# Loading x ahead of the modulation weights, and transposing it two channel tiles ahead of its use

## The chip, the cores and the metric

The kernel runs on one core of one Trainium2 chip. The metric is device time in microseconds (us) of one execution. Below, PE is the matmul engine, DVE, ACT and POOL are the vector, scalar and general engines, and SP is the queue that issues nearly all DMAs.

## The reference, cut to what matters

One layer of an encoder over 512 tokens of 2048 channels, all in float32, with one conditioning vector c:

```python
mod = silu(c) @ w_ada + b_ada                  # 2048 x 12288
sh1, sc1, gt1, sh2, sc2, gt2 = split(mod, 6)
h = rmsnorm(x, g_norm_mix) * (1 + sc1) + sh1
proj = h @ w_in                                # 2048 x 3072: xr, gr (gate), xp (pool)
...                                            # RG-LRU heads and pooling heads, then w_out
x = x + gt1 * y
...                                            # SwiGLU with sh2, sc2, gt2, then a last rmsnorm
```

rmsnorm divides each token's row by the root of its mean square (a factor rstd per token) and multiplies by a weight per channel.

## The kernel before

**How it is written and ordered.** The program lists its operations in order of the mathematics; a class `Program` records them and orders them itself. It gives every operation a cost (`cost`, line 113) and a due time, counted back from the nominal times of PE's matmuls (`deadlines`, line 154), and then places them one by one (`schedule`, line 204): for each engine queue it looks at the operations that are ready, takes the one that can start earliest (due time decides between equal ones), and moves this queue's clock. What is issued is the list in order of the planned starts. Each engine works through its own part of the list in order. All instructions are issued from line 356, so every row of the trace has that line; tiles tell them apart.

Tiles come from pools with a fixed number of buffers: `blk` (names b..., 69 buffers of 128 x 512), `raw` (6) for other weights, `araw` (4 buffers of 512 KB) for the modulation weights, `hi` and `lo` (3 each), and the PSUM banks `acc` (6) and `mm` (2). Buffers of a pool are taken in the program's order; one tile may be taken early only where the rest still fits (`fits`, line 239). Two rules keep buffers free: a `raw` load whose due time lies more than 50 us ahead of its queue's clock is not placed, and far-off operations leave 6 `blk` buffers spare (`buffers`, line 260). DMAs with a `lead` are issued first, in order of the lead.

**The start, around the change.** x is loaded in 16 pieces (four token tiles by four column quarters, `xs[t][q]`, line 466). ACT squares each piece and sums it into `ss1`; from this, DVE and ACT form `rstd1`, one factor per token (line 470). ACT then multiplies each piece by rstd1 in place (line 476), PE transposes it in 128 x 128 blocks against the identity into an `acc` bank, and ACT copies the bank to `xt[k]`, a channel tile of 128 channels by 512 tokens (lines 472 to 479). All 16 channel tiles are done so, one after another, before anything else of the mixer in the program's order.

Scale and shift come from w_ada in nine chunks of one or two channel tiles (`ADA_CHUNKS`, `ada_columns`, line 516): each chunk is 2 or 4 MB through the `araw` buffers; DVE multiplies by c's column and adds up (one instruction per 128 x 256 or 128 x 512, `b<-araw,c_act,b`), PE sums over the partitions by matmuls with a column of ones (`mm<-ones,b`), and DVE writes `gs` and `sh`. `shifted(k)` (line 491) applies them to xt[k] and splits the result into a float32r high part and a low part, h[k]; all products run as three float32r matmuls (high by high, high by low, low by high).

With h[k], PE computes the input projection over the columns in two ways: six column tiles stay in the six `acc` banks over all chunks (`held_job`, line 573, sums over all 16 channel tiles), ten others are summed in groups of channel tiles 0 to 1, 2 to 7 and 8 to 15 through the two `mm` banks (`group_job`, line 583). The eight gate columns follow after the last chunk. The loop over chunks is at lines 749 to 769.

Of the kernel before, what the change touches and what calls it, by code (L numbers as in the profile page):

```python
# [12 lines left out]
AF = mybir.ActivationFunctionType  # L13
ALU = mybir.AluOpType

P = 128
D = 2048
T = 512
NT = T // P
KD = D // P  # L20
# [7 lines left out]
ADA_CHUNKS = (1, 1, 2, 2, 2, 2, 2, 2, 2)  # L28
GROUP_ENDS = (2, 8, 16)
HELD = 6  # L30
NFF = 5632 // 512
DOWN_BLOCKS = (2, 3, 3, 3)
BUFS = {"blk": 69, "raw": 6, "araw": 4, "hi": 3, "lo": 3, "acc": 6, "mm": 2}
# [3 lines left out]
class Program:  # L37
# [166 lines left out]
    def schedule(self):  # L204
        self.dependences()
        self.deadlines()
        ops, tags, bufs = self.ops, self.tags, self.bufs
# [19 lines left out]
        taken, last_use = set(), {}  # L227
        waiting, ready = [len(op["pred"]) for op in ops], [0.0] * len(ops)
        clock = {q: 0.0 for q in self.QUEUES.values()}
        dma_free, table, busy, port = 0.0, None, {}, 0.0  # L230
        start, left = [None] * len(ops), len(ops)
        pace = [op for op in ops if op["q"] == "PE"][::-1]
        shift, wide = 0.0, False
# [26 lines left out]
        def buffers(op, now):  # L260

            need, when = [x[0] for x in op["w"] if x[0] in tags and x[0] not in taken], 0.0
            for name in need:
                tag = tags[name]
                late = op["due"] - shift - now
                if not free[tag] or tag == "raw" and late > self.RAW_AHEAD and not wide:
                    return need, None
                if not fits(name, self.spare.get(tag, 0) if late > self.SPARE_AHEAD else 0):
                    return need, None
                when = max(when, min(free[tag]))  # L270
            return need, when
# [7 lines left out]
        while left:  # L279
            while pace and start[pace[-1]["i"]] is not None:  # L280
                pace.pop()
            shift = pace[-1]["nominal"] - clock["PE"] if pace else shift
            best = {}
            for (q, _), heap in lanes.items():
                now, tried = clock[q], []
                while heap and (wide or len(tried) < self.SCAN):
                    due, i = heapq.heappop(heap)
                    tried.append((due, i))
                    if q == "PE" and pace and ops[i]["nominal"] > pace[-1]["nominal"] + self.AHEAD:
                        continue  # L290
                    need, when = buffers(ops[i], now)
                    if when is None:
                        continue
                    t = max(now, ready[i], when, port if ops[i]["port"] else 0.0)
                    cand = (t, due + 2.0 * (ops[i]["table"] not in (None, table)), i, need)
                    if q not in best or t < best[q][0] - 0.02 or t <= best[q][0] + 0.02 and cand[1] < best[q][1]:
                        best[q] = cand
                    if t <= now and ops[i]["table"] in (None, table):
                        break
                for x in tried:  # L300
                    heapq.heappush(heap, x)
            if not best:
                assert not wide, "no instruction can go"
                wide = True
                continue
            wide = False
            t, _, i, need = min(best.values())
            op = ops[i]
            q = op["q"]
            heap = lanes[lane(op)]  # L310
            heap.remove((op["due"], i))
            heapq.heapify(heap)
            for name in need:
                tag = tags[name]
                free[tag].remove(max([x for x in free[tag] if x <= t] or free[tag]))
                taken.add(name)
                early[tag].append(place[name])
            start[i] = t
            if op["dma"]:
                issue = self.DMA_ISSUE if q == "SP" else self.DMA_BUILD  # L320
                clock[q] = t + issue
                dma_free = max(dma_free, t + issue + self.DMA_START - self.DMA_ISSUE) + op["t"]
                end = dma_free + self.DMA_LAND
            else:
                if op["table"] not in (None, table):
                    t, table = t + self.TABLE_LOAD, op["table"]
                    start[i] = t
                end = t + op["t"]
                if op["port"]:
                    port = max(port, end)  # L330
                if q == "PE":
                    tick = int(t / self.CLOCK_TICK)
                    if busy.get(tick - 1, 0.0) < self.CLOCK_SHARE * self.CLOCK_TICK:
                        end += op["t"]
                    busy[tick] = busy.get(tick, 0.0) + op["stream"]
                clock[q] = end
            op["end"] = end
            left -= 1
            for name in op["tiles"]:
                users[name] -= 1  # L340
                last_use[name] = max(last_use.get(name, 0.0), end + self.LATENCY[q])
                if not users[name]:
                    free[tags[name]].append(last_use[name])
            for j in op["succ"]:
                waiting[j] -= 1
                r = ops[j]["q"]
                ready[j] = max(ready[j], end + (0.0 if r == q == "PE" else self.LATENCY[q] + 0.1 * (r == "PE")))
                if not waiting[j]:
                    push(ops[j])
# [10 lines left out]
def hybrid_trunk(ctx: ExitStack, tc: tile.TileContext, a: dict, out: bass.AP):  # L360
# [6 lines left out]
    nc = Program(tc.nc, BUFS, SPARE)  # L367
    ids = iter(range(1 << 20))
    ts, tt, stt = nc.vector.tensor_scalar, nc.vector.tensor_tensor, nc.vector.scalar_tensor_tensor

    def blk(dt=F32):
        return nc.tile(pool, [P, T], dt, "blk", f"b{next(ids)}")
# [5 lines left out]
    def mmps(tag="mm"):  # L378
        return nc.tile(psum, [P, 512], F32, tag, f"{tag}{next(ids)}")
# [30 lines left out]
    ident = const.tile([P, P], F32, name="ident")  # L410
# [8 lines left out]
    def rows_of(src):  # L419
        return src.rearrange("(r p) -> r p", p=P)  # L420
# [37 lines left out]
    x2 = a["x"][0]  # L458
    xs = [[None] * 4 for _ in range(NT)]
# [3 lines left out]
    for q in range(4):  # L463
        for t in range(NT):
            xs[t][q] = blk()
            nc.sync.dma_start(out=xs[t][q], in_=x2[t * P:(t + 1) * P, q * 512:(q + 1) * 512], lead=(0, 2, 4, 6)[q])
            ss = ss1[:, 4 * t + q:4 * t + q + 1]
            nc.scalar.activation(out=blk(), in_=xs[t][q], func=AF.Square, accum_out=ss)

    rstd1 = rstd_from(ss1, NT, after=sqrt_ready)  # L470
    xt = []
    for k in range(KD):
        ps = mmps("acc")
        for t in range(NT):
            if k % 4 == 0:
                nc.scalar.activation(out=xs[t][k // 4], in_=xs[t][k // 4], func=AF.Copy, scale=rstd1[:, t:t + 1])
            nc.tensor.transpose(out=ps[:, t * P:(t + 1) * P], in_=xs[t][k // 4][:, (k % 4) * P:(k % 4 + 1) * P], identity=ident)
        xt.append(blk())
        nc.scalar.activation(out=xt[k], in_=ps, func=AF.Copy)

# [86 lines left out]
    proj = {}  # L567
    held = {n: mmps("acc") for n in range(HELD)}

# [145 lines left out]
    def pool_group(g):  # L715
# [16 lines left out]
        for j in range(2):  # L732
            ps = mmps()
            for k in range(2):
# [11 lines left out]
                  lead=3)  # L746
    start = 0
    group = 0
    for ci, nk in enumerate(ADA_CHUNKS):
        ada_columns(0, start, nk)  # L750
        end = start + nk
        for k in range(start, end):
            h[k] = shifted(k)
        if end == 8:
            param_columns(cols_b, 72,
                          [a["w_conv"][0].rearrange("i (r p) -> (i r) p", p=P), rows_of(a["b_conv"][0]), rows_of(a["b_rg_a"][0]),
                           rows_of(a["b_rg_i"][0]), rows_of(a["lru_lambda"][0]), a["ls_pool"][0].rearrange("g (r p) -> (g r) p", p=P)])
            sp, spn = softplus()
            bd = [gate_weights(name) for name in ("w_rg_a", "w_rg_i")]
        for n0 in range(0, HELD, 8 // nk):  # L760
            held_job(start, nk, n0, min(8 // nk, HELD - n0))
        if end in GROUP_ENDS and end < KD:
            gk = end - group
            m = max(1, 8 // gk)
            for base, cnt in ((HELD, NL - HELD), (2 * NL, NL)):
                for n0 in range(base, base + cnt, m):
                    group_job(group, gk, n0, min(m, base + cnt - n0))
            group = end
        start = end
# [34 lines left out]
    for q in range(4):  # L804
# [18 lines left out]
        for k in range(4 * q, 4 * q + 4):  # L823
            ps = mmps()
# [148 lines left out]
    wd = a["w_ffn_down"][0].rearrange("(ko p) n -> p ko n", p=P)  # L973
    f_kept = [dram.tile([P, 7 * T], F32, name=f"f{i}") for i in range(2 * NFF)]
    gt2_kept = [dram.tile([P, 512], F32, name=f"gt2_{q}") for q in range(4)]
# [60 lines left out]

    for n in range(NFF):
        keep(n, gate_up(n))
# [146 lines left out]
```

## Time and profile before

| | us |
|---|---|
| median of 3 runs | 1902.73 (1899.97 to 1902.89) |
| profiled execution | 1899.48 |
| its span, first to last instruction | 1897.7 |
| PE busy | 1805.7 (95%) |
| DVE busy | 1544.1 (81%) |
| ACT busy | 930.7 (49%) |
| mean granted PE clock | 0.990 |

The profile is of one execution. Busy time counts instructions; matmuls are pipelined and overlap in it. A row of the timeline gives the start, the time covered and the count of a run of like instructions, and in brackets the engine's idle time before it with what ended it.

### The profile page before, as it was taken

To read this page: it belongs to the slowest core of one execution; us is meant where nothing else is said; L and a number is where in the kernel's file an instruction comes from. 1 tells how busy PE (TensorE), PEld (TensorE's weight loads), DVE (VectorE), ACT (ScalarE), POOL (GpSimd) and SP (SyncE) were. 2 spreads that over 40 slices of the span, in tenths; PEclk is the share of its full clock that TensorE was granted. 3 is DMA by queue.
4 is the path that set the end of the run, shared out by engine and by line. 5 is a ranking of instruction groups with operands and counts; after the bars stand their busy time and mean duration, and the time that the engine had idled before them with its cause. 6 is when DMAs were issued, how large, how long until landed. Compare 5 with 4: busy or idle time off the path is not lost.

```text
span 1897.7 us, 22755 instructions
## 1 busy us (share of the span) xinstructions
PE 1805.7 (95%) x8019; PEld 1471.6 (78%) x8019; DVE 1544.1 (81%) x1978; ACT 930.7 (49%) x1208; POOL 197.8 (10%) x192
## 2 busy tenths in 40 slices
PE   3899999899998999999999999999999999999997
PEld 2687877687776788888888888888887888888875
DVE  5897999889969879687877867877667888888888
ACT  7435784432228455454554545545444543333345
POOL 0000045500000111111111111111110000000011
PEclk9999999999999999999999999999999999999999
DMA  9997455599972688678967878867799765947566
GB/s 295 311 350 231 153 180 178 183 318 313 349 240 47 175 205 233 173 227 220 224 186 211 230 183 218 229 175 198 168 288 355 230 237 184 351 142 254 203 158 166
DMA packets 283587, 425.78 MB, mean 224 GB/s; under 512 B 20632, under 2 KB 119632, under 8 KB 283472
## 3 DMA queue, kind: packets, MB, share of 16 engines
q1 hardware_dynamic: 257232, 373.98, 58.9%
q0 software_dynamic: 26240, 50.34, 15.9%
q8 instruction: 63, 1.03, 0.2%
q14 instruction: 52, 0.43, 0.1%
HBM read 374.44 MB, written 49.81 MB: 224 GB/s over the span
## 4 chain that ended last, share of the span: by engine, by line
PE 73%; DVE 13%; DMA 8%; ACT 3%; issue 3%; SPq 0%; POOL 0%; ACTq 0%; DVEq 0%
PE acc L356 70%; DVE b L356 9%; DMA araw<-in_w_ada 4%; PE mm L356 3%; DVE lo L356 3%; ACT b L356 2%; DMA raw<-in_w_ffn_down 1%; ACT hi L356 1%; DMA raw<-in_w_ffn_up 1%; DMA f<-b 1%; DMA raw<-in_w_ada 1%; DVE araw L356 0%; SPq L356 0%; DMA b<-f 0%; DMA raw<-in_w_in 0%
## 5 line engine op out<-in xcount | busy, mean ns | idle before, releaser
L356 PE MATMUL acc<-hi,b 128*128 128x512 f32 x4208 | 1270.0, 392 | 12.7 <-DVE b L356 6.0
L356 PEld LDWEIGHTS acc<-hi,b 128*128 128x128 f32 x4208 | 789.0, 188 | 179.8 <-DVE b L356 9.1
L356 PE MATMUL acc<-lo,b 128*128 128x512 f32 x2104 | 780.7, 392 | 2.3 <-DVE lo L356 2.3
L356 ACT ACTIVATE hi<-raw 128x1024 fp32r<-128x1024 f32 (+2 forms) x289 | 298.6, 1034 | 472.5 <-PE acc L356 405.1
L356 PEld LDWEIGHTS acc<-lo,b 128*128 128x128 f32 x2104 | 396.1, 188 | 89.5 <-DVE lo L356 8.2
L356 DVE TENSOR_TENSOR lo<-raw,hi 128x1024 fp32r<-128x1024 f32 (+2 forms) x289 | 346.0, 1199 | 135.8 <-ACT hi L356 134.7
L356 ACT ACTIVATE hi<-araw 128x1024 fp32r<-128x1024 f32 x264 | 279.5, 1060 | 282.7 <-PE acc L356 254.5
L356 DVE TENSOR_TENSOR lo<-araw,hi 128x1024 fp32r<-128x1024 f32 x198 | 241.3, 1220 | 54.0 <-ACT hi L356 53.2
L356 DVE SCALAR_TENSOR_TENSOR b<-araw,c_act,b 128x512 f32<-128x512 f32 (+1 forms) x315 | 236.1, 755 | 15.7 <-DMA araw<-in_w_ada 11.3
L356 DVE TENSOR_TENSOR b<-b,b 128x512 f32<-128x512 f32 (+4 forms) x318 | 188.5, 617 | 14.6 <-ACT b L356 14.0
L356 PE MATMUL acc<-b,hi 128*128 128x512 f32 x608 | 188.2, 394 | 5.1 <-ACT b L356 4.4
L356 ACT ACTIVATE b<-b 128x512 fp32r<-128x512 f32 (+2 forms) x223 | 128.7, 595 | 92.4 <-DVE b L356 55.3
L356 PEld LDWEIGHTS acc<-b,hi 128*128 128x128 f32 x608 | 114.1, 189 | 30.7 <-ACT b L356 6.5
L356 POOL DMA_DIRECT2D araw<-in_w_ffn_up x44 | 52.6, 1195 | 621.1 <-DVE lo L356 620.3
L356 PE MATMUL acc<-b,lo 128*128 128x512 f32 x304 | 115.0, 392 | 0.0
L356 ACT ACTIVATE b<-acc 128x512 f32<-128x512 f32 x142 | 82.3, 593 | 56.6 <-PE acc L356 45.9
L356 DVE SCALAR_TENSOR_TENSOR lo<-araw,hi 128x1024 fp32r<-128x1024 f32 x66 | 80.6, 1221 | 36.0 <-ACT hi L356 35.6
L356 DVE TENSOR_TENSOR araw<-araw,raw 128x1024 f32<-128x1024 f32 x88 | 106.6, 1218 | 0.8
L356 DVE SCALAR_TENSOR_TENSOR araw<-araw,raw 128x1024 f32<-128x1024 f32 x66 | 79.8, 1219 | 8.8 <-DMA raw<-in_w_ffn_down 4.5
L356 POOL DMA_DIRECT2D raw<-in_w_ffn_up x44 | 52.5, 1192 | 312.9 <-DVE lo L356 284.9
L356 PE MATMUL mm<-b,hi 128*128 128x512 f32 x192 | 62.8, 408 | 12.3 <-ACT b L356 10.9
L356 DVE TENSOR_TENSOR b<-acc,b 128x512 f32<-128x512 f32 x94 | 61.5, 684 | 15.9 <-PE acc L356 15.7
(75 smaller groups left out, 878.8 us busy)
## 6 DMA issues: line engine op xcount, KB each, us to landing
araw<-in_w_ada SPq DMA_DIRECT2D x256, 256.0 KB, 4.6
raw<-in_w_ffn_down SPq DMA_DIRECT2D x88, 512.0 KB, 5.6
f<-b SPq DMA_DIRECT2D x154, 256.0 KB, 4.1
b<-f SPq DMA_DIRECT2D x154, 256.0 KB, 6.1
raw<-in_w_ffn_up SPq DMA_DIRECT2D x44, 512.0 KB, 4.4
araw<-in_w_ffn_gate SPq DMA_DIRECT2D x44, 512.0 KB, 3.9
araw<-in_w_ffn_up POOLq DMA_DIRECT2D x44, 512.0 KB, 6.7
raw<-in_w_ffn_gate SPq DMA_DIRECT2D x44, 512.0 KB, 5.0
```

The source lines that it names most:

```text
L356: getattr(getattr(self.nc, queue), method)(*args, **kw)
```

## The change

x's last column quarter gets a lead of 4.5 instead of 6, so that it is issued before the first modulation weights (lead 5). The transposes become a function `transposed(k)`, which takes an `mm` bank and is called in the loop over chunks, for all channel tiles up to two beyond the chunk's end. For the first eight channel tiles, x is not scaled first: DVE builds four diagonal blocks of rstd1 (`diag`), and the transpose is a matmul of the unscaled block with the diagonal. The other eight are scaled by ACT and transposed as before. In `schedule`, the clock against which a buffer's lead is counted is at least the latest start placed so far (`today`).

```diff
+XT_AHEAD = 2
+DIAG_TILES = 8
...
-        dma_free, table, busy, port = 0.0, None, {}, 0.0
+        dma_free, table, busy, port, today = 0.0, None, {}, 0.0, 0.0
...
-                    need, when = buffers(ops[i], now)
+                    need, when = buffers(ops[i], max(now, today))
...
             t, _, i, need = min(best.values())
+            today = max(today, t)
...
-            nc.sync.dma_start(out=xs[t][q], in_=x2[t * P:(t + 1) * P, q * 512:(q + 1) * 512], lead=(0, 2, 4, 6)[q])
+            nc.sync.dma_start(out=xs[t][q], in_=x2[t * P:(t + 1) * P, q * 512:(q + 1) * 512], lead=(0, 2, 4, 4.5)[q])
...
     xt = []
-    for k in range(KD):
-        ps = mmps("acc")
+
+    diag = blk()
+    for t in range(NT):
+        ts(out=diag[:, t * P:(t + 1) * P], in0=ident, scalar1=rstd1[:, t:t + 1], scalar2=None, op0=ALU.mult)
+
+    def transposed(k):
+
+        ps = mmps()
         for t in range(NT):
+            tok, x = slice(t * P, (t + 1) * P), xs[t][k // 4]
+            if k < DIAG_TILES:
+                nc.tensor.matmul(ps[:, tok], x[:, (k % 4) * P:(k % 4 + 1) * P], diag[:, tok], start=True, stop=True)
+                continue
             if k % 4 == 0:
-                nc.scalar.activation(out=xs[t][k // 4], in_=xs[t][k // 4], func=AF.Copy, scale=rstd1[:, t:t + 1])
-            nc.tensor.transpose(out=ps[:, t * P:(t + 1) * P], in_=xs[t][k // 4][:, (k % 4) * P:(k % 4 + 1) * P], identity=ident)
+                nc.scalar.activation(out=x, in_=x, func=AF.Copy, scale=rstd1[:, t:t + 1])
+            nc.tensor.transpose(out=ps[:, tok], in_=x[:, (k % 4) * P:(k % 4 + 1) * P], identity=ident)
         xt.append(blk())
         nc.scalar.activation(out=xt[k], in_=ps, func=AF.Copy)
...
         ada_columns(0, start, nk)
         end = start + nk
+        for k in range(len(xt), min(KD, end + XT_AHEAD)):
+            transposed(k)
         for k in range(start, end):
             h[k] = shifted(k)
```

## Rows read from the trace of the kernel before

**Rows 1.** The page's 40 slices of the span, busy tenths of PE.
```profile
PE   3899999899998999999999999999999999999997
```

**Rows 2.** Busy time (instructions) by stretch; last: granted clock, DMA share, GB/s.
```profile
26.00:41.40 15.40, 10.02 (x54) 8.07 (x55) 12.10 (x35) 13.56 (x27) 0.00 (x0) 0.97 1.10 375
41.40:57.00 15.60, 12.20 (x52) 8.00 (x50) 13.30 (x20) 10.09 (x18) 0.00 (x0) 0.92 0.91 284
57.00:79.00 22.00, 19.76 (x82) 15.13 (x83) 18.25 (x30) 10.27 (x17) 0.00 (x0) 0.92 1.01 334
79.00:97.50 18.50, 17.63 (x81) 13.85 (x80) 18.43 (x32) 10.25 (x17) 0.00 (x0) 1.00 0.99 299
97.50:147.80 50.30, 50.30 (x224) 41.27 (x224) 47.96 (x87) 14.88 (x22) 0.00 (x0) 1.00 1.02 341
147.80:151.50 3.70, 1.03 (x9) 0.97 (x8) 3.70 (x10) 2.08 (x4) 0.00 (x0) 1.00 0.99 331
151.50:183.00 31.50, 31.49 (x146) 26.21 (x147) 22.03 (x50) 15.59 (x24) 0.00 (x0) 1.00 0.74 239
```
The order of the five engines in each row is PE, PE's weight loads, DVE, ACT, POOL.

**Rows 3.** Timeline of the SP queue, 11 to 21 us.
```profile
11.42 7.40 SPq L356 DMA_DIRECT2D araw<-in_w_ada  x8
18.86 2.07 SPq L356 DMA_DIRECT2D b<-in_x  x4
```

**Rows 4.** Timeline of PE, 34 to 99 us.
```profile
34.68 1.61 PE L356 MATMUL acc<-ident,b 128*128 128x128 f32 x12 [0.17 <-ACT b L356]
...
41.70 1.20 PE L356 MATMUL acc<-b,hi 128*128 128x512 f32 x2
...
57.13 0.50 PE L356 MATMUL mm<-b,lo 128*128 128x512 f32 x1 [2.70 <-DVE lo L356]
...
93.41 1.02 PE L356 MATMUL mm<-ones,b 128*128 128x1 f32 x8 [0.20 <-DVE b L356]
...
97.50 1.43 PE L356 MATMUL acc<-b,hi 128*128 128x512 f32 x5
```

**Rows 5.** Groups of ACT, 29 to 50 us: busy, mean ns of one, idle before.
```profile
L356 ACT ACTIVATE b<-b,s 128x512 f32<-128x512 f32 x16 | 10.2, 714 | 0.0
L356 ACT ACTIVATE b<-acc 128x512 f32<-128x512 f32 x16 | 8.7, 606 | 0.0
...
L356 ACT ACTIVATE b<-b,sh,gs 128x512 fp32r<-128x512 f32 x1 | 0.8, 813 | 0.0
```

**Rows 6.** The chain of waits that ended last: start, us, what.
```profile
79.59 2.95 DMA araw<-in_w_ada
...
141.64 4.76 DMA araw<-in_w_ada
```

**Rows 7.** Timeline of DVE, 18 to 79 us.
```profile
18.22 0.35 DVE L356 TENSOR_SCALAR b<-araw,c_act 128x256 f32<-128x256 f32 x1 [5.51 <-DMA araw<-in_w_ada]
...
29.41 0.15 DVE L356 SCALAR_TENSOR_TENSOR gs<-gs,cols_a 128x1 f32<-128x1 f32 x1
...
75.20 0.16 DVE L356 TENSOR_TENSOR gs<-mm,cols_a 128x2 f32<-128x2 f32 x1 [1.08 <-PE mm L356]
...
78.68 0.16 DVE L356 TENSOR_TENSOR gs<-mm,cols_a 128x2 f32<-128x2 f32 x1 [1.02 <-PE mm L356]
```

**Rows 8.** Instructions on the tile ident: least, median, greatest ns; first and last.
```profile
L356 DVE TENSOR_SCALAR b<-ident,s x4: 281/285/288, 553.0 to 565.5; 128x128 f32<-128x128 f32 x4
```

**Rows 9.** Timeline of PE near 567 us, a f32 matmul of 128 columns.
```profile
567.22 1.91 PE L356 MATMUL mm<-b,ones 128*128 128x128 f32 x8
```

**Rows 10.** Timeline of PE, 147 to 153 us.
```profile
148.80 1.02 PE L356 MATMUL mm<-ones,b 128*128 128x1 f32 x8 [0.99 <-DVE sh L356]
151.51 1.66 PE L356 MATMUL acc<-b,hi 128*128 128x512 f32 x6 [1.69 <-ACT b L356]
```

**Rows 11.** Busy time by stretch, columns as in rows 2, two later stretches.
```profile
500.00:600.00 100.00, 88.62 (x400) 70.31 (x399) 83.08 (x157) 51.01 (x89) 4.92 (x4) 0.95 0.66 207
...
1800.00:1898.00 98.00, 82.16 (x351) 66.23 (x349) 83.80 (x117) 47.62 (x75) 13.66 (x16) 0.94 0.64 164
```

## The prediction

> **What bounds the kernel now.** I read the page first, for its 40 slices [rows 1]: PE is at 3 tenths in the first slice, then at 8 or 9 of 10 nearly everywhere. What the change touches directly lies in the first four slices, so the next view is the table of busy time by stretch, cut where the PE's work changes its kind [rows 2]. The reader is to see three things in it. First, from 97.5 to 147.8 PE is busy for all of 50.30 us, and from 151.5 to 183 for 31.49 of 31.50: behind 97.5 PE is full. Second, from 57 to 97.5 DVE is nearly as full: 18.25 of 22.00 us, then 18.43 of 18.50. Third, the DMA share is about 1 from 57 to 147.8 (1.01, 0.99, 1.02). So in the first 150 us two streams run beside each other: PE's products, and the stream of the modulation weights (DMA into four araw buffers, DVE's multiply-adds out of them). DVE gives the buffer back, and the next load waits for that.
>
> Then the timelines. The SP queue [rows 3] issues the first eight ada loads at 11.42 and the last four loads of x only at 18.86, so the row scales of all of x are late. PE [rows 4] transposes x before and after 34.68 (this row is a stretch of it without waits, 12 in 1.61 us) and starts its first projection product at 41.70. ACT in the same stretch [rows 5] carries sixteen scaled copies of x, 10.2 us, and evictions of the transposes; it is the engine that holds the transposes back.
>
> The rows that decide what an earlier start is worth come later: at 93.41 PE waits 0.20 us for DVE's sum of the fifth chunk (channel tiles 6 and 7; I number chunks from one), and at 97.50 it goes on with products [rows 4]. From 97.50 on it has work without a break. So PE comes to that point with no backlog: whatever it does earlier than now, it must wait there, unless the fifth chunk comes earlier too. The chain of waits says the same: from 79.59 to 97 it runs over ada loads and DVE, not over PE, and it comes by an ada load again at 141.64 [rows 6].
>
> **The change, part by part.** All sums are made against the profiled execution, 1899.48 us (span 1897.7, 1.8 us around it). The runs shown have a median of 1902.73, 3.25 above; I add the differences to the median. About 0.2%, 3.8 us, is what a measurement can tell from no change.
>
> *x ahead of the ada weights.* Four DMAs of x, 2.07 us of the SP queue, go ahead of eight ada DMAs of 7.40 us [rows 3]. x's squares end some 7 us earlier (18.86 becomes 11.42). Behind them on SP, the first chunk comes 2.07 us later; DVE's first multiply-add starts at about 20.3 instead of 18.22 [rows 7]. The number of loads is the same, and by the end of the second chunk the queue has issued the same bytes. DVE idles 3.3 us in 26 to 41.4 (15.40 less 12.10, [rows 2]), which covers the 2.07 us. Cost 0; without that cover +2.07.
>
> *rstd as a diagonal.* DVE gets four instructions of 0.285 us, as for the diagonal that the kernel builds later [rows 8], 1.14 us; with the 2.07 us this makes 3.2, just inside the 3.3 us of idle time. Cost 0, bounds 0 and +1.14. ACT loses eight of its sixteen scaled copies, 8 x 0.714 = 5.7 us [rows 5]. No gain by itself: ACT is not what is late behind 52 us (10.27 of 22.00 us busy, [rows 2]). PE pays: 32 transposes become matmuls with a 128-column f32 operand. The nearest row has eight of these in 1.91 us, 0.239 each, against 0.134 for a transpose [rows 4, 9]: 32 x 0.105 = 3.4 us. They fall before 92 us, where PE idles 3.4 + 2.2 + 0.9 us from 41.4 to 97.5 [rows 2] and more before, so I take 0; bounds 0 and +3.4.
>
> The Trainium skill, Perfetto Trace Analysis, section Transposes, wants a logical transpose issued as a transpose and not as a standard matmul. The rows agree on the price (0.134 against 0.239 us); by the rule the change would be 3.4 us dearer, a sum of 1905.1, if PE were late there.
>
> *Transposes just in time, over the two mm banks.* Tiles 0 to 2 are transposed for the first chunk instead of all sixteen, and the six acc banks need not be given back by transposes first. The first product needs gs of the first chunk (29.41 + 0.15 now [rows 7], about 31.6 with 2.07 added) and ACT's 0.81 us [rows 5]: about 33 instead of 41.70, so PE starts 8 to 9 us earlier.
>
> Where does that go? From 57 to 79 the chain is PE's (group products through the two mm banks); DVE waits at 75.20 and 78.68 for PE, 1.08 and 1.02 us [rows 7], and in all idles 3.75 us there (22.00 less 18.25). PE ahead by 8 us takes these waits away. Next late is DVE itself: no multiply-add of the ada chunks goes away. So the fifth chunk comes earlier by 0 to 3.75 us; the stretch right after it, where DVE runs at 18.43 of 18.50 with the DMA at 0.99, shows that it can run without such waits, so I take 3.75. The other idle time, 2.3 us in 41.4 to 57, waits for ada loads, which the change does not speed: 0 there, upper bound 2.3.
>
> Against it stands what the moved transposes cost. Tiles 8 to 15 are now transposed behind 93 us, where PE is full: 8 x 4 x 0.134 = 4.3 us. Two of the eight can go into the hole from 147.8 to 151.5, where PE idles 3.70 less 1.03 = 2.67 us while it waits for DVE and ACT [rows 2, 10]; one more can go early into the wait for the fifth chunk, since one mm bank is free then. Five stay: 5 x 0.535 = 2.7 us. Bounds 0 (all in waits) and 4.3. Their evictions (0.606 us each, [rows 5]) run on ACT, which is busy for only 14.88 of 50.30 us there [rows 2].
>
> *The planner's clock.* It lets a queue that stood still count its lead from the latest instruction placed. It can only change the order of loads and of buffer use. PE's idle time outside the start is small and gives the bounds: 11.4 us in 500 to 600 and 15.8 in the last 98 us [rows 11]. I see no reason for a sign: 0, with 3 us either way, a quarter of the first of these.
>
> Sum: -3.75 + 2.7 = -1.05 us, 1902.73 - 1.05 = 1901.7. That is within 0.2%.
>
> **Rivals.** (1) The early start goes through. All DVE idle time before the fifth chunk vanishes (3.75 + 2.3 us), the hole of 2.67 us closes, and the eight tiles fit into waits: -8.7 us, about 1894. For it: DMA moved 375 GB/s from 26 to 41.4 against 284 from 41.4 to 57 [rows 2], so the loads have room once ACT and DVE are rid of the transposes. Against it: DVE's work stays, 49.98 us of the 56.1 from 41.4 to 97.5, and it would have to run without a gap.
>
> (2) Slower: the transposes decide. If the fifth chunk does not come earlier (DVE is late by x's 2.07 us and never makes up for it), all eight late tiles stay on a full PE, 4.3 us. On top, PE, now ahead, idles before the fifth chunk; after its idle 2.70 us at 57.13 [rows 4] the granted clock of 57 to 79 is 0.92, 8% of 22 us = 1.8 us, for stretches at the lower of its levels. Together +6.1, 1908.8. It decides as soon as the fifth chunk gains less than 2.3 us (6.1 less 3.8). With the diagonal's 3.4 us on the path too it would be 1912.2; of this rival's chance that is 0.04. The Trainium skill's rule on transposes (above) speaks for this side; the trace agrees with its price, and shows no full PE where the diagonal falls.
>
> (3) The re-planned order moves a later stretch by some 6 us, twice the bound taken, either way: 1896 or 1908. The page speaks against much of it, since PE is at 9 tenths in nearly all later slices [rows 1].
>
> **Chances.** Forecast 0.45 (within 0.2%: 0.37; its ends beyond: 0.05 faster, 0.03 slower). Rival 1 0.28, all faster. Rival 2 0.17, all slower. Rival 3 0.10: 0.04 faster, 0.02 within, 0.04 slower. So faster 0.37, same 0.39, slower 0.24. The forecast's own terms go from -6.05 (late tiles all in waits, ada waits gone too) to +4.3, 1896.7 to 1907.0; to leave out no more than 2 in 10, the range takes in most of rivals 1 and 2: 1893 to 1908.5.
>
> **What would show it.** Right: the first product at 33 to 34 us; ada loads starting near 13.5; DVE's waits for PE at 75 to 79 gone; PE idle for several us before the fifth chunk, whose sum reaches PE 2 to 4 us before 93.41; transposes among PE's products behind 93 us; the 500th and the 1400th us showing the same work within 3 us. Wrong: the fifth chunk earlier by more than 6 us, or not at all; PE waiting for an mm bank behind a transpose; the hole near 148 us gone; or the shift at 200 us not being the shift at the end, which would put the cause into the later order.

## The result and the profile after

The changed kernel takes 1914.25 us (median of 5 runs, 1908.98 to 1916.21); the kernel before, run beside it, 1902.89 (1899.97 to 1908.44). The ratio is 1.0053, 95% interval 1.0027 to 1.0079: slower by some 10 us, where no change was forecast and 1908.5 was the upper end. The profiled execution took 1913.98 us with a span of 1912.2, 14.5 more than the span before, so single profiles overstate the loss by a few us. I use the profiles for places and the ratios for sizes.

The SP queue of the changed kernel, 8 to 33 us (start, time covered, count), answers to [rows 3]:

```profile
8.90 4.83 SPq L359 DMA_DIRECT2D b<-in_x  x8
13.78 8.77 SPq L359 DMA_DIRECT2D araw<-in_w_ada  x8
22.59 2.15 SPq L359 DMA_DIRECT2D raw<-in_w_in  x4
24.86 1.39 SPq L359 DMA_DIRECT2D araw<-in_w_ada  x2
...
```

Eight ada loads fill the four araw buffers. Before, x's last four loads then stood in the queue while DVE worked its way to the first free buffer, and the ninth ada load went out at 21.05. Now x is gone from there, four w_in loads stand in that place, and the ninth ada load goes out at 24.86.

DVE's timeline (with the idle time before a row and what ended it): the first multiply-adds of the first six chunks, the reduction for rstd1 that stands ahead of them, one of the splits of w_in between them, and the longest wait on an ada load, in the second chunk; answers to [rows 7].

```profile
20.98 0.17 DVE L359 TENSOR_REDUCE s<-s 128x4 f32<-128x16 f32 x1 [8.46 <-ACT b L359]
...
21.79 0.35 DVE L359 TENSOR_SCALAR b<-araw,c_act 128x256 f32<-128x256 f32 x1
...
30.61 0.96 DVE L359 TENSOR_TENSOR lo<-raw,hi 128x768 fp32r<-128x768 f32 x1 [0.48 <-ACT hi L359]
...
33.28 0.35 DVE L359 TENSOR_SCALAR b<-araw,c_act 128x256 f32<-128x256 f32 x1 [0.33 <-DMA araw<-in_w_ada]
...
42.37 1.52 DVE L359 SCALAR_TENSOR_TENSOR b<-araw,c_act,b 128x256 f32<-128x256 f32 x3 [2.08 <-DMA araw<-in_w_ada]
...
44.94 0.48 DVE L359 TENSOR_SCALAR b<-araw,c_act 128x512 f32<-128x512 f32 x1
...
61.61 0.47 DVE L359 TENSOR_SCALAR b<-araw,c_act 128x512 f32<-128x512 f32 x1
...
76.04 0.48 DVE L359 TENSOR_SCALAR b<-araw,c_act 128x512 f32<-128x512 f32 x1
...
95.68 0.48 DVE L359 TENSOR_SCALAR b<-araw,c_act 128x512 f32<-128x512 f32 x1
```

The same six rows before start at 18.22 [rows 7], 28.00, 37.84, 54.01, 70.40 and 92.12. The modulation stream is late by 3.6, 5.3, 7.1, 7.6, 5.6 and 3.6 us: the delay grows over two chunks, and half of it is made good. That it grows has a place on DVE: the first chunk's sixteen multiply-adds end at 32.96, 11.2 us after their start, where before they take 8.2 (18.22 to 26.38). The new order puts the end of rstd1, the four diagonal blocks and three splits of w_in (`lo<-raw,hi`) between them.

PE's timeline, answers to [rows 4] and [rows 10]:

```profile
33.01 1.01 PE L359 MATMUL mm<-ones,b 128*128 128x1 f32 x4 [6.49 <-DVE b L359]
33.89 3.63 PE L359 MATMUL mm<-b,b 128*128 128x128 f32 x16
...
37.27 0.70 PE L359 MATMUL acc<-b,hi 128*128 128x512 f32 x2
...
45.96 0.58 PE L359 MATMUL mm<-ones,b 128*128 128x1 f32 x4 [3.45 <-DVE b L359]
...
93.55 0.60 PE L359 MATMUL mm<-ident,b 128*128 128x128 f32 x4
96.97 1.02 PE L359 MATMUL mm<-ones,b 128*128 128x1 f32 x8 [2.82 <-DVE b L359]
...
150.90 0.63 PE L359 MATMUL mm<-ident,b 128*128 128x128 f32 x4
153.61 1.22 PE L359 MATMUL acc<-b,hi 128*128 128x512 f32 x2 [2.08 <-ACT b L359]
154.63 1.06 PE L359 MATMUL mm<-ident,b 128*128 128x128 f32 x4
...
164.71 1.03 PE L359 MATMUL mm<-ident,b 128*128 128x128 f32 x8
```

The first chunk's sum reaches PE at 33.01, before at 26.53. The first product is 4.4 us earlier (37.27 against 41.70), and none of it is left at the fifth chunk. PE waits 3.45 us for the second chunk's sum and 2.82 us for the fifth's, which comes at 96.97 instead of 93.41. One tile of the late transposes lies in that wait (93.55); the others come behind it, most of them in stretches that were full of products before.

Busy time by stretch, columns and stretches of [rows 2]:

```profile
26.00:41.40 15.40, 8.91 (x40) 7.93 (x41) 12.92 (x29) 7.05 (x11) 0.00 (x0) 1.00 1.03 338
41.40:57.00 15.60, 11.39 (x43) 8.71 (x43) 13.08 (x22) 3.79 (x6) 0.00 (x0) 0.78 0.91 301
...
97.50:147.80 50.30, 49.73 (x222) 40.95 (x222) 48.55 (x99) 16.74 (x25) 0.00 (x0) 0.97 1.02 340
147.80:151.50 3.70, 3.60 (x18) 2.59 (x17) 3.70 (x10) 0.00 (x0) 0.00 (x0) 1.00 0.99 325
```

From 26 to 41.4 DMA moved 338 GB/s, against 375 before: 0.57 MB less in that stretch, though the loads there were to be covered. ACT is down from 13.56 to 7.05 us, as meant. The hole that lay at 147.8 to 151.5 before is filled there and comes 2 us later instead: PE waits 2.08 us ahead of 153.61.

A marker for the following: the first Sigmoid's table load on ACT, the first work behind the projection, stands at 209.11 before and at 215.75 after. In these two profiles 6.6 us are lost by then, 3.6 at the fifth chunk's sum and 3.1 between it and the Sigmoid.

Some of the kernels below run the same instructions in the same order on every engine up to about 195 us, and so show how far one profile fixes these two places. The start of before was profiled three times (before itself, its start with the change's rest, and the planner's clock alone; all below): the fifth sum is at 93.41, 91.29 and 91.48, the first Sigmoid at 209.11, 208.80 and 207.02. The change's start twice: 96.97 and 99.17, then 215.75 and 217.38. The start with x behind twice: 92.01 and 92.44, then 210.79 and 214.14. So one pair of profiles can't tell a difference of 2 us in the fifth sum, or of some 3 us in the Sigmoid, from none. By these profiles the change's loss up to the first Sigmoid is 6.6 to 10.4 us.

### The profile page after: what moved, and what is told of

Its sections match the earlier page's. It is cut to its first block, busy times and chain, and to the rows that moved or that the text cites. A ratio compares the mean times of both kernels' runs of the same rounds, so it can differ in the third digit from the quotient of the medians.

```text
span 1912.2 us, 22832 instructions
## 1 busy us (share of the span) xinstructions
PE 1816.5 (95%) x8051; PEld 1485.2 (78%) x8051; DVE 1540.1 (81%) x1982; ACT 926.4 (48%) x1200; POOL 195.2 (10%) x192
## 3 DMA queue, kind: packets, MB, share of 16 engines
q8 instruction: 63, 1.03, 0.2%
## 4 chain that ended last, share of the span: by engine, by line
PE 69%; DVE 13%; DMA 9%; ACT 5%; issue 3%; SPq 1%; POOL 1%; ACTq 0%; DVEq 0%; POOLq 0%
PE acc L359 64%; DVE b L359 8%; PE mm L359 5%; DVE lo L359 4%; DMA f<-b 3%; ACT b L359 2%; DMA araw<-in_w_ada 2%; ACT L359 1%; ACT hi L359 1%; DMA raw<-in_w_ffn_gate 1%; DVE araw L359 1%; DMA b<-in_x 1%; DMA raw<-in_w_ffn_down 1%; SPq L359 1%; DMA b<-f 1%
## 5 line engine op out<-in xcount | busy, mean ns | idle before, releaser
L359 DVE TENSOR_TENSOR b<-b,b 128x512 fp32r<-128x512 f32 (+5 forms) x318 | 189.0, 617 | 16.5 <-ACT b L359 13.6
L359 ACT ACTIVATE b<-acc 128x512 f32<-128x512 f32 x126 | 73.7, 592 | 65.0 <-PE acc L359 46.0
L359 PE MATMUL mm<-b,hi 128*128 128x512 f32 x192 | 63.4, 415 | 12.0 <-ACT b L359 11.2
```

Source lines behind the costliest of these rows:

```text
L359: getattr(getattr(self.nc, queue), method)(*args, **kw)
```

## The experiments

Where a run keeps an order, the operations are issued by a written list instead of by the planner: "the order of before behind the first Sigmoid" is that list's second part. All ratios are against runs of the kernel before on the same chip (medians there 1905.88, 1906.57 and 1905.04 us in the three sets of four). Theory A: the order of the loads costs. Theory B: the late transposes among PE's products cost. Theory C: the planner's new order of the later part costs.

**x in front alone.** The kernel before, its own order written out, with one edit (a sketch of the list; nothing else moves in it):

```diff
-  issue order: ... x (4 loads) | w_ada (8) | x (last 4) | w_ada ...
+  issue order: ... x (8 loads) | w_ada (8) | w_ada ...
```

> The kernel before in its own order, instruction by instruction, with one thing changed: the last four loads of x stand ahead of the first eight ada loads on SP. Theory A (load order: behind the first chunk, x's four loads filled the time in which the second chunk's loads wait for DVE to give back an araw buffer; ahead of it they only delay the chunk): DVE's first multiply-add goes from 18.2 to about 21.5, the fifth chunk's sum reaches PE about 3 us after 93.4, and the whole takes 3 to 5 us longer than before. Theory B (the transposes among PE's products cost the time): no difference from before beyond 1.5 us, the fifth chunk at 93 to 94. Theory C (the time goes in the later part, through the re-planned order): no difference from before.

1.0026 (1.0009 to 1.0043). DVE's first multiply-adds of the first three chunks, and PE's sum of the fifth:

```profile
21.89 0.35 DVE L454 TENSOR_SCALAR b<-araw,c_act 128x256 f32<-128x256 f32 x1 [9.44 <-DMA araw<-in_w_ada]
30.70 0.34 DVE L454 TENSOR_SCALAR b<-araw,c_act 128x256 f32<-128x256 f32 x1
39.23 0.48 DVE L454 TENSOR_SCALAR b<-araw,c_act 128x512 f32<-128x512 f32 x1
...
95.96 1.02 PE L454 MATMUL mm<-ones,b 128*128 128x1 f32 x8 [1.92 <-DVE b L454]
```

So A holds by itself: about half of the change's loss is here, with no other part of it present. The first multiply-add is 3.7 us late and the fifth sum 2.6 (4.7 against the earliest profile of the same order). In between the delay shrinks, to 2.7 us at the second chunk and 1.4 at the third; at the fourth it is 2.4 again. So here the chunks' delay does not grow as it does in the change. The ninth ada load goes out at 23.83, where before it followed x's loads at 21.05, and SP's longest wait for DVE to give back a buffer is 3.7 us instead of 2.2. Since the order is kept, rstd1 stays behind the first chunk on DVE (29.97 against 26.87), and the first product comes 2.4 us later too (44.10); that is part of this run's price.

**x behind, the rest of the change kept.** Planned anew:

```diff
-...lead=(0, 2, 4, 4.5)[q])
+...lead=(0, 2, 4, 6)[q])
```

> The changed kernel with x's last quarter behind the first ada loads again (lead 6), planned anew. Theory A: the first multiply-add is back near 18.2, the fifth chunk's sum at 93 to 94 instead of 96.97, the first Sigmoid table load 4 to 6 us earlier than 215.75, the whole 4 to 6 us below the changed kernel. Theory B: the start of the stream comes earlier but the first Sigmoid table load stays within 2 us of 215.75, and so does the whole of the changed kernel's time. Theory C: within 3 us of the changed kernel.

1.0006 (0.999 to 1.0022). The first multiply-add is back at 18.23 and the first product comes at 36.01, 5.7 us earlier than before. PE's sum of the fifth chunk and what follows it, then DVE's waits from 60 to 77 us:

```profile
92.01 1.84 PE L359 MATMUL mm<-ones,b 128*128 128x1 f32 x8 [5.25 <-DVE b L359]
93.71 1.09 PE L359 MATMUL mm<-ident,b 128*128 128x128 f32 x4
```
```profile
60.92 1.54 DVE L359 SCALAR_TENSOR_TENSOR b<-araw,c_act,b 128x512 f32<-128x512 f32 x2 [0.95 <-DMA araw<-in_w_ada]
...
72.63 2.08 DVE L359 SCALAR_TENSOR_TENSOR b<-araw,c_act,b 128x512 f32<-128x512 f32 x3 [0.31 <-DMA araw<-in_w_ada]
76.26 2.32 DVE L359 SCALAR_TENSOR_TENSOR b<-araw,c_act,b 128x512 f32<-128x512 f32 x3 [0.65 <-DMA araw<-in_w_ada]
```

This is A's course, and more: 0.47% or some 9 us below the changed kernel, where A had said 4 to 6. Even with the load order mended, PE's lead ends in a wait of 5.25 us at the fifth chunk. DVE no longer waits for PE there, but for ada loads instead, and the fifth sum, at 92.01, lies among the three of the start of before (91.29 to 93.41): it gains nothing that can be told.

**The two halves of the order.** First the change's start up to the first Sigmoid with the order of before behind it, then the reverse: the kernel before up to the first Sigmoid, and the change's order behind it.

> The changed kernel up to the first Sigmoid in its own order, everything behind it in the order of the kernel before, written out. Theories A and B (all is lost in the start and only carried on): 11 us slower than before, as the changed kernel. Theory C: the start's 6 to 7 us stay, the other 5 to 8 go away: 6 to 7 us slower than before.

> The kernel before up to the first Sigmoid in its own order, everything behind it in the order of the changed kernel. Theories A and B: as before, within 2 us. Theory C: 5 to 8 us slower than before, with the same start to within 1 us (first Sigmoid table load at about 209).

1.0040 (1.0024 to 1.0056) and 1.0014 (0.9998 to 1.003). Most of the loss goes with the start, some 7.6 us; that lies between the 11 of theories A and B and the 6 to 7 of C. The later order's 0.14%, some 2.7 us, lies between their numbers too, and its interval takes in no change at all.

**The planner's clock alone**, in the kernel before (the three lines with `today`, planned anew):

> The kernel before with the planner's new clock alone (the line with today). Theory C (the later order costs a little of its own): start as before, first Sigmoid at 208 to 210 us, ratio 1.001 to 1.003. Theory A alone (all of the loss is in the first 100 us): ratio 0.999 to 1.001.

1.0008 (0.9993 to 1.0022), with the first Sigmoid at 207.02, earlier than either side expected, though up to 195 us the order is that of before. The interval holds both theories' numbers; the point lies below C's. Theory C is not shown, and not ruled out.

**Five araw buffers, x in front.** The changed kernel with

```diff
-BUFS = {"blk": 69, "raw": 6, "araw": 4, ...
+BUFS = {"blk": 67, "raw": 6, "araw": 5, ...
```

> The changed kernel with five araw buffers instead of four; for the room, blk has 67 instead of 69, and the order is planned anew. Theory A1 (the loss is the wait for an araw buffer: with x in front, nothing fills the time until DVE gives the first buffer back): the first multiply-add stays at 21.8 us, since its bytes still come behind x, but the third chunk starts on DVE at 39 to 41 us instead of 44.94, the first Sigmoid comes at 210 to 212 us instead of 215.75, and the ratio to the kernel before is 1.001 to 1.003 (changed kernel 1.0053). Theory A2 (the loss is x's 1 MB by itself, carried ahead of the first chunk, and the buffers have no part in it): the third chunk stays at 44 to 45, the first Sigmoid at 215 to 216, the ratio at 1.004 to 1.006. The two blk buffers less can cost some us later in either case.

1.0061 (1.0043 to 1.0078): by the time this is A2's case, not A1's. The places point the other way. SP's waits from 18 to 60 us (us in total, times, longest) on DVE's use of a buffer, in the changed kernel and then with five buffers:

```profile
SPq L359 <- DVE b L359: 11.2, 14, 3.8
```
```profile
SPq L359 <- DVE b L359: 8.0, 14, 1.4
```

DVE's first multiply-adds of the first three chunks, and ACT's first Sigmoid, with five:

```profile
22.56 0.35 DVE L359 TENSOR_SCALAR b<-araw,c_act 128x256 f32<-128x256 f32 x1
29.18 0.35 DVE L359 TENSOR_SCALAR b<-araw,c_act 128x256 f32<-128x256 f32 x1 [0.77 <-DMA araw<-in_w_ada]
39.97 0.48 DVE L359 TENSOR_SCALAR b<-araw,c_act 128x512 f32<-128x512 f32 x1 [0.18 <-DMA araw<-in_w_ada]
```
```profile
207.86 1.28 ACT L359 ACT_TABLE_LOAD   x1
```

The first chunk is as late as in the change (x's bytes still come first), but the third starts at 39.97 instead of 44.94, and the first Sigmoid is 7.9 us earlier than in the change. These are A1's signs. They do not show A1, for DVE's order changed with the buffers: here the second chunk begins after eleven of the first chunk's sixteen multiply-adds, and the splits of w_in come later. On PE the first chunk's sum is no earlier (33.62 against 33.01), the second's by 1.8 us (44.17 against 45.96), the fifth's by 5.2 (91.79 against 96.97). No run gives the kernel before a fifth buffer. So that the wait for a buffer, more than the new order, keeps x's bytes from being made good is argued. The run loses its lead again later. PE from 600 to 1000 us in the changed kernel and in this one:

```profile
600.00:1000.00 400.00, 393.47 (x1754) 321.57 (x1753) 321.36 (x387) 209.20 (x258) 47.67 (x40) 1.00 0.75 193
```
```profile
600.00:1000.00 400.00, 386.48 (x1715) 316.78 (x1714) 311.39 (x370) 200.05 (x243) 47.67 (x40) 0.99 0.74 193
```

PE idles 7.0 us more there, and 6.8 more from 1000 to 1400. That the two blk buffers given up cause this is likely, but the order changed too, so it is argued only.

**The place of the late transposes.** x behind, and the loop over chunks as in the diff; behind the first Sigmoid the order of before (the edit beside the lead of 6):

```diff
-        for k in range(len(xt), min(KD, end + XT_AHEAD)):
+        for k in range(len(xt), min(KD, end + (XT_AHEAD if end < 6 else 10))):
```

> The change with x's last quarter behind the first ada chunk, as before, and with all late channel tiles transposed by the fifth chunk instead of two ahead; from the first Sigmoid on, the order of the kernel before, written out. Theory B (what is left of the loss is the eight late tiles' transposes, which lie among the products on a full PE behind 97 us; ahead of the fifth chunk PE idled 5.25 us with x behind): the transposes go into that idle time, the first Sigmoid comes at 206.5 to 208 us (x behind alone 210.79, before 209.11), and the ratio is 0.998 to 1.000. Rival (the modulation stream alone sets the fifth chunk and all behind it, and the transposes hide in waits anyway): first Sigmoid 210 to 211, ratio 1.000 to 1.001.

0.9973 (0.9962 to 0.9985), faster than the kernel before, and by a little more than theory B had said; the first Sigmoid, at 208.67, is a little later than it had said. To hold this against the same kernel with the transposes left late, that was run too:

> The change with x's last quarter behind the first ada chunk, transposes two ahead as the change has them, and from the first Sigmoid on the order of the kernel before, written out. It differs from the run with early transposes (0.9973) by the place of the late transposes alone, and from the run with x behind (1.0006) by the later order alone. Theory B (the late transposes among full PE cost): first Sigmoid at 210 to 211 us, ratio 0.999 to 1.000, 0.1 to 0.2% above the run with early transposes. Rival C (the later order made that difference): ratio within 0.0007 of 0.9973.

1.0014 (0.9996 to 1.0031). The place of the transposes is the only edit between the two, and they are 0.41% apart, some 7.8 us: theory B, and more than it had said. PE at the fifth chunk's sum, time of all instructions on the identity's tile from 92 to 190 us (PE's is the first busy figure), and the first Sigmoid; transposes late, then early:

```profile
86.84 0.60 PE L456 MATMUL mm<-ident,b 128*128 128x128 f32 x4
92.44 1.84 PE L456 MATMUL mm<-ones,b 128*128 128x1 f32 x8 [5.00 <-DVE b L456]
94.14 1.09 PE L456 MATMUL mm<-ident,b 128*128 128x128 f32 x4
```
```profile
92.00:190.00 98.00, 5.22 (x29) 4.24 (x29) 0.00 (x0) 0.00 (x0) 0.94 0.85 277
```
```profile
214.14 1.28 ACT L456 ACT_TABLE_LOAD   x1
```
```profile
92.71 1.02 PE L457 MATMUL mm<-ones,b 128*128 128x1 f32 x8 [0.17 <-DVE b L457]
```
```profile
92.00:190.00 98.00, 0.23 (x1) 0.14 (x1) 0.00 (x0) 0.00 (x0) 0.98 0.87 286
```
```profile
208.67 1.28 ACT L457 ACT_TABLE_LOAD   x1
```

Both reach the fifth sum together. The late ones then put 5.0 us of transposes on PE (5.22 less 0.23), and the first Sigmoid is 5.5 us later in this pair of profiles, 2.1 in the other profile of the same start (x behind, 210.79). The early ones lie at 77 to 87 us, and the products that they push back fill the time in which the other kernel's PE idles for 5.00 us. The planner orders the start anew around them, so the two differ in more than the 32 instructions: the first product, for one, comes at 36.09 and 38.80.

**x in front with early transposes.** The edit above with lead 4.5:

> The change as it is, x in front, but all late channel tiles transposed by the fifth chunk; from the first Sigmoid on the order of the kernel before. Theories A and B together (two separate costs): the load order's 3 to 5 us stay, the late transposes' 2 to 4 us go: first Sigmoid at 212 to 214 us (change 215.75, with the old rest 217.38), ratio 1.001 to 1.003 (with the old rest 1.0040). Rival (the transposes cost only where x is behind; with x in front DVE alone sets the time): first Sigmoid 216 to 218, ratio 1.0035 to 1.0045.

1.0005 (0.999 to 1.0019), a little better than expected; the first Sigmoid comes at 210.71, also earlier than the 212 to 214 expected. With this run there are four corners, all with the order of before behind the first Sigmoid:

| ratio to before | transposes late | transposes early |
|---|---|---|
| x in front | 1.0040 | 1.0005 |
| x behind | 1.0014 | 0.9973 |

The load order costs 0.26 and 0.32%, the late transposes 0.35 and 0.41%: two separate costs that add. For three of the four steps the intervals on both sides don't touch. For the load order's 0.26% they do (1.0024 to 1.0056 beside 0.9996 to 1.0031), but the run with x in front alone gave 0.26% as well. 1.0040 and 0.9973 were measured on one chip, the other two on a second one, each against the kernel before on the same chip; a difference between the chips would raise one price of a pair as much as it lowers the other, so the means, 0.29 and 0.38%, are free of it. Each price is that of the edit with the order that the planner makes of it: with x in front, the fourth chunk starts on DVE at 57.93 with early transposes and at 62.56 with late ones, well ahead of the late ones' place.

**All late transposes one chunk earlier still** (x behind, with the third chunk):

> As the run with x behind and early transposes (0.9973), but all late channel tiles are transposed one chunk earlier, with the third chunk. Theory B (any place before the fifth chunk is free, since PE waits there for DVE): within 0.0007 of 0.9973. Other side (there PE's group products hold up DVE through the two mm banks): 0.998 or more.

0.9975 (0.996 to 0.9991): both places before the fifth chunk cost the same. This run shares its chip with the 1.0014 of the late ones, so on one chip too early and late are 0.39% apart.

**The diagonal**, taken out of the changed kernel, and out of the fast corner (`DIAG_TILES = 0`):

> The changed kernel without the diagonal: all x scaled by ACT and transposed against the identity, order planned anew. Theory A (the load order decides; the diagonal is small): DVE is rid of 4 x 0.28 us between the first chunk's multiply-adds, so the chunks come 0 to 1.2 us earlier; first Sigmoid 214 to 216 us, ratio 1.004 to 1.006. Rival (the diagonal is a good part of the loss, by its 32 f32 matmuls at 0.23 us and its DVE instructions in front of the multiply-adds): first Sigmoid 3 us or more earlier, ratio below 1.004. Other side (ACT's scaled copies hold up the start): first product later than 39 us, ratio above 1.006.

> As the run with x behind and early transposes (0.9973), but without the diagonal: ACT scales all of x, and all blocks are transposed against the identity. If the diagonal costs (1.14 us of DVE, 3.4 us of PE before the fifth chunk, both now nearly full there): ratio 0.995 to 0.997. If ACT's eight further copies hold up the first products instead: 0.998 to 1.000. If neither: within 0.0007 of 0.9973.

1.0046 (1.0029 to 1.0063) beside 1.0053, and 0.9968 (0.9954 to 0.9981) beside 0.9973. In both places the kernel without the diagonal is ahead by less than the intervals can tell: no cost of the diagonal is measured, but one of up to some 0.2% is not excluded, and 0.9968 lies in the range that was given for a cost as well as in that for none. The places lean to a small cost. In the fast corner the first Sigmoid comes 5 us earlier without it:

```profile
203.72 1.28 ACT L457 ACT_TABLE_LOAD   x1
```

In the changed kernel the fifth sum comes 3.2 us earlier without it (93.80), though the Sigmoid does not (215.60). ACT's eight further copies held nothing up: the first product came at 36.19, with the diagonal at 37.27.

The diagonal's price on PE was read too high. In the changed kernel, sixteen of its matmuls and, below, the stretch around them (granted clock third from the end):

```profile
83.58 1.95 PE L359 MATMUL mm<-b,b 128*128 128x128 f32 x16
```
```profile
83.50:85.60 2.10, 2.10 (x19) 2.02 (x18) 2.06 (x4) 2.10 (x5) 0.00 (x0) 1.00 1.07 336
```

That is 0.122 us each, against 0.129 for the eight transposes in 1.03 us at 164.71; from start to start it is 0.111 and 0.109. The row from which the prediction took 0.239 [rows 9] stands in a stretch at half the clock, in the kernel before:

```profile
567.00:569.20 2.20, 2.20 (x11) 1.94 (x10) 0.00 (x0) 0.03 (x1) 0.00 (x0) 0.50 1.00 204
```

At the start, from 33.89, they did take 0.227 each. The trace's record of the granted clock begins only at 37.25 us, at the upper level. Up to 37.23 the sixteen start 0.21 us apart, about twice the 0.111 above, so PE was by this at the lower level until then; the 1.00 that the table gives for 26 to 41.4 says nothing of the time before 37.25.

## Why the prediction was wrong, point by point

**The step that failed first: "x ahead of the ada weights", cost 0.** The price was taken from the time that SP needs to issue four loads, 2.07 us [rows 3]; what counts is the data. Four loads of 256 KB come ahead of the first chunk, 1.05 MB, and the first multiply-add moved by 3.7 us with x in front alone, where DVE waits for the load. (In the change it moved by 3.6; there DVE's wait ends on ACT at 20.98, since rstd1 now stands ahead of it.) The Trainium skill (Perfetto Trace Analysis, section What "DMA-bound" means) says of an issuing engine's track that it shows the making of descriptors and not the movement of data; the two numbers here, 2.07 us of issue and a shift of 3.7, agree with it. The cover, DVE's 3.3 us of idle time, held for a while only: with x in front alone the delay falls to 1.4 us at the third chunk and is 2.4 again at the fourth. x's loads had stood, before, while SP waited for DVE to give back a buffer, and cost little there; with them gone, the ninth ada load still goes out 2.8 us later. "By the end of the second chunk the queue has issued the same bytes" was wrong: the change moved 0.57 MB less from 26 to 41.4. What makes the delay grow to 7.1 us in the change is a further step that the prediction lacked, DVE's other work among the first chunk's multiply-adds. Measured for the load order: 0.26 to 0.32%, 5 to 6 us.

**The step that carried the sum: the fifth chunk 3.75 us earlier.** DVE's two waits for PE did go, as forecast. But the step asked what is late next and answered "DVE itself". It was the ada loads as well: with x behind, DVE waits 0.95, 0.31 and 0.65 us for them in the stretch where it waited for PE. The DMA share of 1.01 in that stretch [rows 2] was read in the first part and not carried into this one. Whether those loads were late by their bytes or by the return of buffers stays open; with x behind, the share from 57 to 79 us was 0.96. In the change the fifth sum came 3.6 us later, not 3.75 earlier; with x behind it gained nothing that can be told (92.01 and 92.44 beside 91.29 to 93.41).

**The late transposes: 2.7 us.** The mechanism was right and the size was off. Two of the places that it named did take a tile: in the run that isolates them, four transposes at 86.84 lie in the wait for the fifth chunk and four at 148.87 in the hole near 148. The other six tiles, not five, lie among products or right behind the fifth sum, and the 28 transposes behind 92 us took 5.0 us of PE time, 0.18 each instead of 0.134; the four at 94.14 took 1.09 us at half the clock. The edit as a whole cost 0.35 to 0.41%, 6.7 to 7.8 us. The wait for the fifth chunk, 2.8 to 5.2 us long, had room for more, but "two ahead" doesn't issue them there; placed by the fifth chunk they take that room.

**The sum.** With both costs taken out, the kernel is 0.27% or some 5 us faster than before, about the gain that the forecast had booked (3.75). That the size fits is no proof of its place: the fifth sum of that run is at 92.71, no earlier than before. The load order adds 5 to 6 us, the late transposes 7, the later order some 3 (not clear of noise): together the change's 10.

**Rival 2** named this course: the fifth chunk not earlier since DVE never makes up for x, the eight tiles all on a full PE, PE idle before the fifth chunk and then at a lower clock. It was given 0.17 and 1908.8 us. It lacked the load order's own price: "does not come earlier" turned out to be 3.6 us later.

**What was right.** The diagonal at 0, within what the runs can tell, and by luck in part: its 3.4 us on PE rested on a row at half the clock. The Trainium skill's rule against a matmul in place of a transpose (Perfetto Trace Analysis, section Transposes) gains no time that these runs show: at the same clock, 0.122 us for the matmul against 0.129 for the transpose, and no difference that could be told from noise between the kernels with and without the diagonal. The planner's clock at 0 within 3 us fits 1.0008. The first product was expected at 33 to 34 and came at 37.27; with x behind it came at 36.01, without the diagonal at 36.19. In the change it follows straight on the sixteen matmuls by the diagonal that start at 33.89, on a PE still at the lower clock.

**What stays open.** By the first Sigmoid, at least 6.6 us are lost in the profiles, against the change's 10 in all. Behind it, profiles of single executions of the same order differ by several us among themselves, so I can't say at which wait the rest goes. Nor do the profiles show where the fast corner gains its 0.27%: its first Sigmoid is 0.4 us earlier than before, and its span is the same 1897.7; the profiled execution of before, 1899.48 us, was faster than the median of the later sets by 6 us.

## What to carry to other kernels

A load that stands in a queue right behind those that fill the last free buffer may cost next to nothing there: moved forward, it cost its bytes here, and the wait that it had filled stayed. When a wait is taken from an engine, look at the share of every resource in that stretch before booking its length as gain; here the DMA share stood at 1.0, and waits for loads came in its place. Deferred work belongs ahead of the wait that the deferral itself opens up, not next to its use on an engine that is full from there on. And before a place in one profile is compared with another, profile the same order twice: here it moved by 2 to 3 us.

## What the runs showed of the hardware that had not been expected

A wait of several us on PE was paid twice here. Granted clock by stretch (the figure behind the five engines) around the fifth chunk's sum, first with PE idle for 5.00 us ahead of 92.44, then with 0.17 us ahead of 92.71:

```profile
92.00:95.50 3.50, 2.80 (x12) 2.42 (x12) 2.91 (x8) 0.23 (x1) 0.00 (x0) 0.50 1.12 362
95.50:99.00 3.50, 3.08 (x8) 2.50 (x9) 2.63 (x8) 2.81 (x5) 0.00 (x0) 0.50 1.11 368
```
```profile
92.00:95.50 3.50, 2.91 (x17) 2.02 (x15) 3.48 (x9) 0.69 (x1) 0.00 (x0) 1.00 1.07 355
```

Behind the long wait PE runs at the lower of its two levels (1.2 GHz) for the 7 us shown, behind the short one at the upper. The eight ones-matmuls take 1.84 us there against 1.02, and four transposes 1.09 against the 0.60 at 86.84. In the changed kernel the same follows the wait of 3.45 us that ends at 45.96 (0.78 from 41.4 to 57) and the wait of 2.08 that ends at 153.61 (0.54 from 153.6 to 157); the four transposes at 154.63 take 1.06 there.
